# A hybrid decoder layer: row products moved from the first to the second attention pass, and a reordered seam in the MLP

## The chip, the cores and the metric

One core of a Trainium2 chip. The metric is the device time in microseconds of one execution, a median of several runs. The core has five engines with a queue of instructions each: TensorE (PE; its weight loads are shown apart as PEld), VectorE (DVE), ScalarE (ACT), GpSimd (POOL) and SyncE (SP, which here only issues DMAs).

## What is computed

One layer with a mixer and an MLP, both in float32. 512 tokens, 2048 columns, 16 heads of 64, 8192 hidden columns. Six rows of 2048 numbers modulate the layer ("modulation rows", 0 to 5 in the kernel):

```python
c_act = jax.nn.silu(c)
mod = c_act @ w_ada + b_ada                    # six rows of 2048
sh1, sc1, gt1, sh2, sc2, gt2 = split(mod, 6)
h = rms_norm(x, g_pre_mix) * (1.0 + sc1) + sh1
proj = h @ w_in                                # q, k, v, gates, recurrent branch
o_att = nsa_attention(...)                     # compressed, selected and window branch
o_rnn = gelu(yr) * rg_lru(conv(xr))
mix = concat(rms_norm(o_att), rms_norm(o_rnn)) @ w_out
x = x + gt1 * rms_norm(mix, g_post_mix)
h = rms_norm(x, g_pre_mlp) * (1.0 + sc2) + sh2
f = square(relu(h @ w_ff1)) @ w_ff2
x = x + gt2 * rms_norm(f, g_post_mlp)
```

`gt1` is row 2, `sh2` row 3, `sc2` row 4 and `gt2` row 5: none of the four is needed before the output projection is evaluated, the last one not before the end of the MLP.

## The kernel before, in words

**Precision.** A float32 operand is split into a high part (a copy by ScalarE in a shorter format) and a low part (the difference, by VectorE), and TensorE makes three products of them. So each weight tile costs ScalarE and VectorE a pass: lines 102 and 103 for the weights of the projections (class `Units`: SyncE loads `wr`, line 84, the split goes to `sl`), lines 1299 and 1300 (`part`) for those of the MLP (`fr`, loaded at line 1294, and sums of its blocks `fs`, lines 1315 to 1318). `AH` and `AL` are the two parts of the activations.

**Row products.** Modulation rows 2 to 5 are not matrix products on TensorE. `qdot` (lines 208 to 219) loads a 128x512 tile of `w_ada` into `md` (line 217), with a quarter of the activated condition in `ca` (line 216, one load for every 16 tiles), and VectorE multiplies and sums them in one instruction (line 218), which in the trace has two records, the product and the read of its sum. 64 such products make a row, 256 make the four. They are put in wherever the program calls `qdot`: in attention (rows 2, 4, 3 in this order), in the output projection (`cdots`, what is left of rows 4 and 3), and in the second MLP product (row 5, one for each step). `qvec` (line 221) adds up a row when it is complete.

**Attention.** `attention(pair, natoms)` runs twice, pass 0 and pass 1, over 64 units (head, branch, 128 query rows): scores on TensorE, a softmax row on VectorE (line 736) with the exponential on ScalarE, a reciprocal and a gate (lines 746, 747), transposes on TensorE, the split of the transposed probabilities (line 767), and the product with the values. Between them `fill` puts pieces of the remaining projections and of the recurrent branch. At the end of each step of the loop `nmod` grows by `MRATE`, 0.8, and a `qdot` is called for each whole unit:

```python
nmod[0] += MRATE
while nmod[0] >= 1:
    qdot(bp, 2 if QD[2] else 4 if QD[4] else 3, 1)
    nmod[0] -= 1
```

**Output projection.** Four blocks of 512 columns (`out_k`, `mmt`: lines 915 to 917), with `cdots` spreading the rest of the products over the first blocks, in the ring `tmp` of six buffers.

**MLP.** The first product (`group`) and the second (`f2_mm`) use a scheme of seven products for a 2x2 block, so that sums of weights and of activations are formed on VectorE. The loop at the end of the program goes over the groups `GR`: first those of ff1 (kinds "a", "b", "c", four groups for one pair of column blocks), then the steps of ff2 (kind "f"; `WIN` and `JOIN` say which pairs belong to which window k). When a pair of ff1 is complete, `pair_end` (lines 1392 to 1423) evacuates its banks, applies relu and square, and stores the seven sums to `ud` on GpSimd's queue. `u_load` (1434) reads them back as `uf` on the same queue, `u_form` (1444 on ScalarE, 1445 on VectorE) splits them into a slot of `AH` and `AL`. `bank_open` (1457) fills a bank of PSUM with zeros before ff2 accumulates in it, `bank_out` (1462) copies it out, `fin_step` finishes the last four windows. The "seam" is the passage from the last pair of ff1 to the first step of ff2; the last pair's `pair_end` runs there in pieces, one after each group.

**What sets the order.** The tile framework schedules the program: each engine has its own queue, filled in an order that follows the written one but is shifted by the framework's readiness estimates, and a buffer of a ring is reused when its last reader is done. A DMA stands in the queue of the engine that issues it, and what is behind it waits if it has to wait.

## Time and profile before

| | |
|---|---|
| runs | 2198.32 us median of 3 (2195.87 to 2200.69) |
| the profiled execution | 2199.99 us, span 2198.3 us |
| mean granted clock of TensorE | 0.982 |
| TensorE busy | 2093.1 us, 95% of the span |
| VectorE busy | 1879.1 us, 85% |
| ScalarE busy | 1392.2 us, 63% |
| GpSimd busy | 63.5 us, 3% |
| moved by DMA | 411.12 MB, 187 GB/s on average |

The share of a span says little of a stage: the page's 40 slices show stretches in which TensorE is busy throughout, and others where VectorE is. All times below are counted from the start of the span. The softmax rows of pass 0 run from 215.7 to 417.6 and those of pass 1 from 482.3 to 652.5; the output projection ends at about 870; the seam lies around 1530. "Granted clock" 1.00 is TensorE's upper level of 2.4 GHz and 0.50 the lower one, 1.2 GHz.

### The profile page before, as it was taken

The numbers are of one execution on the slowest core, as the hardware profiler recorded it, in microseconds if no ns is written. First come the engines' busy times: TensorE is split into PE (matmuls) and PEld (weight loads), VectorE is DVE, ScalarE is ACT, GpSimd is POOL, SyncE is SP. The second block draws the span as 40 slices with busy tenths as digits, with TensorE's granted clock in tenths as the row PEclk, the third lists the DMA queues.
The fourth block names the chain that finished last, engine by engine and source line by source line (L and its number), as shares of the span: only waits on it lengthen the run. The fifth ranks groups of instructions, "written<-read, shape, count | busy, mean of one in ns | idle before, by whom it ended". The sixth has DMA issues, their size and how long they took to land.

```text
span 2198.3 us, 39410 instructions
## 1 busy us (share of the span) xinstructions
PE 2093.1 (95%) x14621; PEld 1911.7 (87%) x14621; DVE 1879.1 (85%) x3764; ACT 1392.2 (63%) x2536; POOL 63.5 (3%) x119
## 2 busy tenths in 40 slices
PE   7998999989999989999999999998999999999995
PEld 3686777778877867899999999998999999999995
DVE  8987989877887677889999999999888887887788
ACT  4349879648995226765555555545766777767764
POOL 0000000000000000000000000000000000000010
PEclk9999999999999999999999999999999999999998
DMA  9764544762127886555555555566766544544453
GB/s 380 309 234 139 189 158 149 219 199 68 59 85 225 275 290 203 180 191 175 184 180 171 175 186 178 194 206 207 248 218 217 188 164 141 165 151 157 138 171 116
DMA packets 138818, 411.12 MB, mean 187 GB/s; under 512 B 18225, under 2 KB 25281, under 8 KB 134273
## 3 DMA queue, kind: packets, MB, share of 16 engines
q1 hardware_dynamic: 126178, 341.49, 46.6%
q0 software_dynamic: 12448, 67.12, 8.8%
q8 instruction: 115, 1.88, 0.4%
q14 instruction: 77, 0.63, 0.1%
HBM read 366.58 MB, written 41.97 MB: 186 GB/s over the span
## 4 chain that ended last, share of the span: by engine, by line
PE 52%; issue 26%; DVE 12%; ACT 5%; DMA 5%; POOL 0%; SPq 0%; DVEq 0%; POOLq 0%; ACTq 0%
PE ps_pj L1132 3%; PE ps_pj L1133 3%; PE ps_pj L1134 3%; DMA md<-wada 3%; DVE fl L1300 3%; PE ps_pj L1479 2%; PE ps_pj L1480 2%; PE ps_pj L1481 2%; PE ps_T L1132 2%; PE ps_T L1134 2%; PE ps_T L1133 2%; PE ps_S L1134 2%; PE ps_S L1132 2%; PE ps_S L1133 2%; PE ps_S L1479 2%
## 5 line engine op out<-in xcount | busy, mean ns | idle before, releaser
L1299 ACT ACTIVATE fh<-fs 128x1024 fp32r<-128x1024 f32 x256 | 272.9, 1066 | 324.7 <-DVE fs L1318 139.6
L1300 DVE TENSOR_TENSOR fl<-fs,fh 128x1024 fp32r<-128x1024 f32 x256 | 312.3, 1220 | 98.2 <-ACT fh L1299 95.7
L1299 ACT ACTIVATE fh<-fr 128x768 fp32r<-128x768 f32 (+2 forms) x296 | 217.1, 735 | 67.5 <-PE ps_pj L1133 13.3
L1300 DVE TENSOR_TENSOR fl<-fr,fh 128x768 fp32r<-128x768 f32 (+2 forms) x296 | 239.9, 814 | 11.3 <-ACT fh L1299 11.3
L102 ACT ACTIVATE sl<-wr 128x512 fp32r<-128x512 f32 (+2 forms) x252 | 145.6, 606 | 150.7 <-DMA wr<-wout 93.4
L218 DVE SCALAR_TENSOR_TENSOR md<-md,ca 128x512 f32<-128x512 f32 x256 | 171.4, 685 | 62.8 <-DMA md<-wada 39.7
L103 DVE TENSOR_TENSOR sl<-wr,sl 128x512 fp32r<-128x512 f32 (+2 forms) x252 | 163.6, 662 | 47.8 <-ACT sl L102 32.7
L1315 DVE TENSOR_TENSOR fs<-fr 128x512 f32<-128x512 f32 x256 | 175.2, 684 | 5.8 <-DMA fr<-wff 4.1
L1479 PE MATMUL ps_pj<-fh,AH 128*128 128x256 f32 x602 | 169.1, 281 | 1.1 <-ACT ps_pj L1459 1.0
L1480 PE MATMUL ps_pj<-fl,AH 128*128 128x256 f32 x602 | 169.1, 281 | 0.0
L1481 PE MATMUL ps_pj<-fh,AL 128*128 128x256 f32 x602 | 168.8, 281 | 0.0
L177 PE MATMUL ps_pj<-AH,sl 128*128 128x512 f32 x384 | 161.7, 421 | 0.1
L179 PE MATMUL ps_pj<-AH,sl 128*128 128x512 f32 x384 | 153.1, 399 | 0.7 <-DVE sl L103 0.7
L178 PE MATMUL ps_pj<-AL,sl 128*128 128x512 f32 x384 | 153.2, 399 | 0.0
L1479 PEld LDWEIGHTS ps_pj<-fh,AH 128*128 128x128 f32 x602 | 113.9, 189 | 2.1 <-ACT ps_pj L1459 2.1
L1480 PEld LDWEIGHTS ps_pj<-fl,AH 128*128 128x128 f32 x602 | 114.0, 189 | 0.4 <-DVE fl L1300 0.4
L1481 PEld LDWEIGHTS ps_pj<-fh,AL 128*128 128x128 f32 x602 | 114.0, 189 | 0.0
L1480 PE MATMUL ps_S<-fl,AH 128*128 128x256 f32 x394 | 110.4, 280 | 2.8 <-DVE fl L1300 2.8
L1479 PE MATMUL ps_S<-fh,AH 128*128 128x256 f32 x394 | 110.5, 280 | 1.3 <-ACT ps_S L1459 1.2
L1318 DVE TENSOR_TENSOR fs<-fs,fr 128x256 f32<-128x256 f32 x256 | 107.6, 420 | 3.5
L1481 PE MATMUL ps_T<-fh,AL 128*128 128x256 f32 x396 | 110.6, 279 | 0.0
L1479 PE MATMUL ps_T<-fh,AH 128*128 128x256 f32 x396 | 110.6, 279 | 0.0
(633 smaller groups left out, 7283.8 us busy)
## 6 DMA issues: line engine op xcount, KB each, us to landing
fr<-wff SPq DMA_DIRECT2D x276, 512.0 KB, 3.7
md<-wada SPq DMA_DIRECT2D x256, 256.0 KB, 4.3
uf<-ud POOLq DMA_DIRECT2D x32, 896.0 KB, 4.9
wr<-win SPq DMA_DIRECT2D x48, 512.0 KB, 3.7
ada<-wada SPq DMA_DIRECT2D x22, 1024.0 KB, 10.2
wr<-wout SPq DMA_DIRECT2D x36, 512.0 KB, 4.9
ud<-uf POOLq DMA_DIRECT2D x18, 896.0 KB, 5.2
ud<-uf POOLq DMA_DIRECT2D x14, 768.0 KB, 4.9
```

Source lines behind the costliest of these rows:

```text
L103: self.nc.vector.tensor_sub(lo, raw, self.f(hi))
L177: T.matmul(o, wh, mh, start=start, stop=False)
L218: (V.scalar_tensor_tensor(w, w, 0.5, CA[0], op0=OP.mult, op1=OP.mult, accum_out=dq[s_][:, q_, k:k + 1]))
L1132: T.matmul(o, wh, b[0], start=start, stop=False, skip_group_check=True)
L1133: T.matmul(o, wh, b[1], start=False, stop=False, skip_group_check=True)
L1134: T.matmul(o, wl, b[0], start=False, stop=stop, skip_group_check=True)
L1299: A.activation(hi, src, AF.Copy)
L1300: V.tensor_sub(lo, src, f(hi))
L1315: V.tensor_add(v2(Sm[:, :512]), v2(R[:, 256:768]), R[:, None, :256].to_broadcast([128, 2, 256]))
L1479: T.matmul(o, uh, hi, start=first and k < 4 and t_ == 0, stop=False, skip_group_check=True)
L1480: T.matmul(o, uh, lo, start=False, stop=False, skip_group_check=True)
L1481: T.matmul(o, ul, hi, start=False, stop=last, skip_group_check=True)
```

## The change

1. **Attention.** `MRATE` becomes a pair of rates, `MR = (0.4, 1.7)`: 0.4 calls of `qdot` per step in pass 0, 1.7 in pass 1. In pass 1 every fourth product takes its factor 0.5 not as a constant but from a fifth column of the current unit's `sm`, which a memset on VectorE fills just before; so the product depends on that tile.
2. **ff2.** Row 5 no longer goes through `qdot`. `q5_load` issues the loads of a product two steps ahead of `q5_dot`, with three buffers for `md` (two before) and two for `ca` (one before), from the window `KQ = 6` on. The store of the finished row and the load of `gbc2` that follows go from SyncE's to GpSimd's queue. The scratch `sq2` moves into the pool `gp`, which opens only then.
3. **Seam.** For the last pair the evacuation of the pair before it, the start of its own `pair_end` and the opening of the seven ff2 banks are written right behind its last group, ahead of the next weight load and of the split of the first activations.

```diff
--- before.py
+++ after.py
@@ -28,8 +28,9 @@
 Q_REST, K_REST, XR_T, YR_T = 0, 6, 8, 16
 
 
-NA1, NA2, NMS, NTMP, NXI, NPC, NSB, TD, MRATE, NMD, NRT = 4, 10, 22, 6, 4, 2, 11, 3, 0.8, 4, 6
+NA1, NA2, NMS, NTMP, NXI, NPC, NSB, TD, MR, NMD, NRT = 4, 10, 22, 6, 4, 2, 11, 3, (0.4, 1.7), 4, 6
 JOIN = [2, 1, 1, 1] * 5 + [2, 1, 1, 0, 3]
+KQ = 6
 HALF, CA_ = 512, 1
 PX = 0
 NB2 = 24
@@ -205,7 +206,7 @@
     CA = {}
     cad = dram.tile([1, D], F32, name="cad")
 
-    def qdot(pool, s_, n, ring=("md", NMD)):
+    def qdot(pool, s_, n, ring=("md", NMD), half=0.5):
         for _ in range(min(n, len(QD[s_]))):
             k, q_ = QD[s_].pop(0)
             w = pool.tile([128, S], F32, name="md", tag=ring[0], bufs=ring[1])
@@ -215,7 +216,7 @@
                 row = cad[0, S * q_:S * q_ + S]
                 nc.sync.dma_start(ca, bass.AP(tensor=row.tensor, offset=row.offset, ap=[[0, 128], [1, S]]))
             nc.sync.dma_start(w, wada[s_, k, :, S * q_:S * q_ + S])
-            (V.scalar_tensor_tensor(w, w, 0.5, CA[0], op0=OP.mult, op1=OP.mult,
+            (V.scalar_tensor_tensor(w, w, half, CA[0], op0=OP.mult, op1=OP.mult,
                                                             accum_out=dq[s_][:, q_, k:k + 1]))
 
     def qvec(o, s_, base=None, plus=0.0):
@@ -732,7 +733,7 @@
         n = 128 * (ch + 1)
         sp_ = UN[u][0]
         p_ = bp.tile([128, S], F32, name="pp", tag="pp", bufs=TD + 1)
-        sm = bp.tile([128, 4], F32, name="sm", tag="sm", bufs=6)
+        sm = bp.tile([128, 5], F32, name="sm", tag="sm", bufs=6)
         V.tensor_tensor_reduce(p_[:, :n], sp_[:, :n], mask[:, S - n:], scale=-0.125, scalar=3e38,
                                op0=OP.add, op1=OP.min, accum_out=sm[:, 0:1])
         A.activation(p_[:, :n], p_[:, :n], AF.Exp, bias=sm[:, 0:1], scale=-1.0, accum_out=sm[:, 1:2])
@@ -942,7 +943,7 @@
         add(lambda k=k: pre_out(k))
     n3 = len(stream)
 
-    nmod = [0.0]
+    nmod, ndot = [0.0], [0]
 
     def attention(pair, natoms):
         seq, info = [], {}
@@ -986,9 +987,14 @@
                 pv(u[0], u[1], i, PC[pair, ep])
                 if u[1] == 1:
                     head_out(u[0], i, t)
-            nmod[0] += MRATE
+            nmod[0] += MR[pair]
             while nmod[0] >= 1:
-                qdot(bp, 2 if QD[2] else 4 if QD[4] else 3, 1)
+                half = 0.5
+                if pair and get(s_) and ndot[0] % 4 == 0:
+                    half = UN[get(s_)][1][:, 4:5]
+                    V.memset(half, 0.5)
+                qdot(bp, 2 if QD[2] else 4 if QD[4] else 3, 1, half=half)
+                ndot[0] += 1
                 nmod[0] -= 1
         fill(natoms - done)
 
@@ -1480,6 +1486,24 @@
             T.matmul(o, uh, lo, start=False, stop=False, skip_group_check=True)
             T.matmul(o, ul, hi, start=False, stop=last, skip_group_check=True)
 
+    Q5, QC = {}, {}
+
+    def q5_load(i):
+        if i >= 64:
+            return
+        k_, q_ = QD[5][i]
+        if k_ == 0:
+            QC[q_] = OPP["p"].tile([128, S], F32, name="ca", tag="ca", bufs=2)
+            row = cad[0, S * q_:S * q_ + S]
+            nc.sync.dma_start(QC[q_], bass.AP(tensor=row.tensor, offset=row.offset, ap=[[0, 128], [1, S]]))
+        Q5[i] = OPP["p"].tile([128, S], F32, name="md", tag="md", bufs=3)
+        nc.sync.dma_start(Q5[i], wada[5, k_, :, S * q_:S * q_ + S])
+
+    def q5_dot(i):
+        k_, q_ = QD[5][i]
+        w = Q5.pop(i)
+        V.scalar_tensor_tensor(w, w, 0.5, QC[q_], op0=OP.mult, op1=OP.mult, accum_out=dq[5][:, q_, k_:k_ + 1])
+
     Y, XT, FIN = {}, {}, {}
 
     def fin_step(k, i):
@@ -1490,7 +1514,7 @@
         def done(t_, j, half):
             Y[n, j, half] = t_
             for c_ in range(2):
-                A.activation(sq2[:, c_], t_[:, 256 * c_:256 * c_ + 256], AF.Square,
+                A.activation(gbc2[1][:, c_], t_[:, 256 * c_:256 * c_ + 256], AF.Square,
                              accum_out=ssqf[:, 2 * j + c_, 2 * n + half:2 * n + half + 1])
             g_ = gbc2[0][:, None, 1024 * half + 256 * n:1024 * half + 256 * n + 256]
             V.scalar_tensor_tensor(v2(t_), v2(t_), (1.0, -1.0)[half], g_.to_broadcast([128, 2, 256]),
@@ -1555,7 +1579,6 @@
                 op_ = pool(ctx, "op")
                 for i in range(3):
                     p_tiles(op_, i)
-                sq2 = op_.tile([128, 2, 256], F32, name="sq2")
                 SL[4] = [(AHf[:, 7168:], ALf[:, 7168:]),
                          tuple(op_.tile([128, 768], F32R, name="us4" + x) for x in "hl")]
                 qst = ExitStack()
@@ -1600,20 +1623,33 @@
                 if g == pairs[-1] and k < NP - 1:
                     for i in (0, 2, 6):
                         x_tile(P[n][i])
-            if qn < 64:
+            if k >= KQ and qn < 66:
+                q5_load(qn)
+                if qn >= 2:
+                    q5_dot(qn - 2)
                 qn += 1
-                qdot(OPP["p"], 5, 1, ("md", 2))
-            elif qn == 64:
+            elif qn == 66:
                 qn += 1
                 qvec(gg2, 5, V_GQF)
-                nc.sync.dma_start(ggd[1].rearrange("o (a p) -> (o p) a", p=128), gg2)
+                G.dma_start(ggd[1].rearrange("o (a p) -> (o p) a", p=128), gg2)
                 qst.close()
-                gbc2[0] = pool(ctx, "gp").tile([128, D], F32, name="gbc2")
-                row_in(gbc2[0], ggd[1])
+                gp = pool(ctx, "gp")
+                gbc2[0] = gp.tile([128, D], F32, name="gbc2")
+                gbc2.append(gp.tile([128, 2, 256], F32, name="sq2"))
+                G.dma_start(gbc2[0], bass.AP(tensor=ggd[1].tensor, offset=ggd[1].offset, ap=[[0, 128], [1, D]]))
             continue
         if g == 2:
             pair_begin(q, kind)
         group(s)
+        if q == QO[-1] and g == 3:
+            for x in pe:
+                for _ in x:
+                    pass
+            pe = [pair_end(q, kind)]
+            next(pe[0])
+            next(pe[0])
+            for i in range(7):
+                bank_open(0, i)
         raw_load(s + 3)
         if s + 2 < len(GR) and GR[s + 2][0] != "a" and not RP:
             for _ in tg_:
@@ -1635,10 +1671,11 @@
                 alpha_end(q, BK.pop((kind, q))[0], ap_, "ax", 2)
             continue
         lastp = q == QO[-1]
-        for x in pe:
-            next(x, None)
-            if lastp:
+        if not (lastp and g == 3):
+            for x in pe:
                 next(x, None)
+                if lastp:
+                    next(x, None)
         if g == 0 and QO.index(q) and PORD[QO.index(q) - 1] == ("b", NA - 1):
             ast.close()
             xst = rst.enter_context(ExitStack())
@@ -1650,9 +1687,8 @@
             if lastp:
                 u_form(QO[0], "x")
                 u_load(QO[1])
-            pe = [pair_end(q, kind)]
-            next(pe[0])
-            if lastp:
+            else:
+                pe = [pair_end(q, kind)]
                 next(pe[0])
     rs = op_.tile([128, 4], F32, name="rsf")
     V.reduce_sum(rs, ssqf, axis=AX.X)
```

Lines of the changed kernel are higher by one in attention and by six in the MLP: 219, 737 and 768 are 218, 736 and 767 of before, and 1305, 1306, 1404, 1405, 1450, 1451 and 1463 are 1299, 1300, 1398, 1399, 1444, 1445 and 1457. Line 995 is the new memset, 1498, 1500 and 1505 are the loads of `ca` and `md` and the product in ff2.

VectorE in pass 1 before, in the middle of the pass: softmax rows (736, with its read), splits of probabilities (767), the normalisation (746, 747), and the convolution of the recurrent branch (805), no row product.

```order
L736 ISA pp,sm<-ps_S,mask 128x384
L736 ISA sm 128x1
L767 TENSOR_TENSOR ptl<-ps_T,pth 128x3x128
L805 SCALAR_TENSOR_TENSOR xc<-xp,vecs,xc 128x512
L746 RECIPROCAL sm<-sm 128x1
L805 SCALAR_TENSOR_TENSOR xc<-xp,vecs,xc 128x512
L747 TENSOR_TENSOR sm<-sm,gates 128x1
L736 ISA pp,sm<-ps_S,mask 128x512
L736 ISA sm 128x1
L805 SCALAR_TENSOR_TENSOR xc<-xp,vecs,xc 128x512
```

The same engine in pass 1 of the change, in its first part; 219 is the row product, 995 the memset into `sm`.

```order
L219 SCALAR_TENSOR_TENSOR md,dq_91<-md,ca 128x512
L747 RECIPROCAL sm<-sm 128x1
L219 SCALAR_TENSOR_TENSOR md,dq_91<-md,ca 128x512
L748 TENSOR_TENSOR sm<-sm,gates 128x1
L768 TENSOR_TENSOR ptl<-ps_T,pth 128x4x128
L737 ISA pp,sm<-ps_S,mask 128x512
L737 ISA sm 128x1
L104 TENSOR_TENSOR sl<-wr,sl 128x512
L995 MEMSET sm 128x1
L737 ISA pp,sm<-ps_S,mask 128x128
L737 ISA sm 128x1
```

Row products now stand between the softmax rows and the splits of pass 1.

VectorE at the seam before, from the split of the second activation tile (1445, `AL`) to that of the third; 1300 splits a weight, 1315 to 1318 are sums of weights, 1399 to 1405 evacuate the last pair of ff1.

```order
L1445 TENSOR_TENSOR AL<-uf,AH 128x1792
L1300 TENSOR_TENSOR fl_17133<-fs,fh_17132 128x1024
L1300 TENSOR_TENSOR fl_17189<-fr,fh_17188 128x768
L1315 TENSOR_TENSOR fs<-fr 128x512
L1399 TENSOR_TENSOR uf<-ps_T,uf 128x2x256
L1317 TENSOR_TENSOR fs<-fs,fr 128x256
L1402 TENSOR_TENSOR uf<-ps_S,uf 128x512
L1300 TENSOR_TENSOR fl_17191<-fs,fh_17190 128x1024
L1404 TENSOR_TENSOR uf<-ps_T,uf 128x2x256
L1405 TENSOR_TENSOR uf<-ps_S,uf 128x256
L1318 TENSOR_TENSOR fs<-fs,fr 128x256
L1445 TENSOR_TENSOR AL<-uf,AH 128x1792
```

The same place of the change.

```order
L1505 SCALAR_TENSOR_TENSOR md,dq_94<-md,ca 128x512
L1306 TENSOR_TENSOR fl_17238<-fr,fh_17237 128x768
L1321 TENSOR_TENSOR fs<-fr 128x512
L1405 TENSOR_TENSOR uf<-ps_T,uf 128x2x256
L1323 TENSOR_TENSOR fs<-fs,fr 128x256
L1408 TENSOR_TENSOR uf<-ps_S,uf 128x512
L1306 TENSOR_TENSOR fl_17240<-fs,fh_17239 128x1024
L1410 TENSOR_TENSOR uf<-ps_T,uf 128x2x256
L1411 TENSOR_TENSOR uf<-ps_S,uf 128x256
L1324 TENSOR_TENSOR fs<-fs,fr 128x256
L1321 TENSOR_TENSOR fs<-fr 128x512
L1451 TENSOR_TENSOR AL<-uf,AH 128x1792
```

The split of the second tile (now 1451) stood four rows ahead of line 1399 and now stands eight rows behind it (line 1405), and a row product (1505) stands ahead.

SyncE at the start of ff2 before: `ca` is the quarter of the condition, `md` the tile of a row product, `fr` the weights of the MLP, each row one DMA (or as many as it says).

```order
L1294 DMA fr<-wff 128x1024 x5
L216 DMA ca<-cad 128x512
L217 DMA md<-wada 128x512 x2
L1294 DMA fr<-wff 128x1024
L217 DMA md<-wada 128x512
L1294 DMA fr<-wff 128x1024 x2
L217 DMA md<-wada 128x512 x2
```

The same queue of the change.

```order
L1300 DMA fr<-wff 128x1024 x5
L1498 DMA ca<-cad 128x512
L1500 DMA md<-wada 128x512 x3
L1300 DMA fr<-wff 128x1024
L1498 DMA ca<-cad 128x512
L1500 DMA md<-wada 128x512
L1300 DMA fr<-wff 128x1024 x2
L1500 DMA md<-wada 128x512 x3
```

A second `ca` is loaded shortly behind the first, and three tiles of `md` stand ahead of the first weight load in place of two.

## Rows read from the trace of the kernel before

**Rows 1.** The page's first part: TensorE's busy time, share of the span, instructions.
```profile
PE 2093.1 (95%) x14621; PEld 1911.7 (87%) x14621; DVE 1879.1 (85%) x3764; ACT 1392.2 (63%) x2536; POOL 63.5 (3%) x119
```

**Rows 2.** Stretches: length; busy PE, PEld, DVE, ACT, POOL; granted clock; DMA share; GB/s.
```profile
215.70:417.60 201.90, 192.61 (x980) 155.34 (x980) 188.52 (x618) 166.82 (x394) 3.95 (x7) 1.00 0.55 173
417.60:482.30 64.70, 59.54 (x367) 52.56 (x365) 47.33 (x125) 25.62 (x52) 0.54 (x1) 0.98 0.72 237
482.30:652.50 170.20, 165.13 (x850) 134.44 (x849) 140.74 (x443) 152.51 (x360) 3.24 (x6) 0.99 0.21 66
...
738.00:870.00 132.00, 122.33 (x534) 95.67 (x533) 96.00 (x241) 52.90 (x124) 0.00 (x0) 0.96 0.77 257
1420.00:1525.00 105.00, 100.80 (x844) 99.96 (x843) 95.61 (x173) 54.82 (x76) 3.74 (x7) 1.00 0.67 222
1525.00:1560.00 35.00, 30.90 (x227) 30.20 (x226) 30.42 (x42) 25.71 (x43) 3.18 (x6) 0.85 0.67 238
1560.00:1740.00 180.00, 172.22 (x1451) 170.18 (x1450) 159.18 (x276) 124.32 (x186) 4.23 (x8) 1.00 0.64 209
1740.00:2100.00 360.00, 360.00 (x3079) 359.81 (x3078) 290.75 (x389) 262.52 (x373) 14.66 (x25) 1.00 0.48 159
...
672.00:805.00 133.00, 131.48 (x567) 104.59 (x567) 95.51 (x220) 42.81 (x83) 0.54 (x1) 1.00 0.82 276
```

**Rows 3.** The same stretches for line 218 alone: VectorE's busy us and rows.
```profile
215.70:417.60 201.90, 48.97 (x145) 1.00 0.55 173
417.60:482.30 64.70, 26.74 (x80) 0.98 0.72 237
482.30:652.50 170.20, 0.00 (x0) 0.99 0.21 66
...
738.00:870.00 132.00, 42.23 (x128) 0.96 0.77 257
```

**Rows 4.** VectorE's timeline (start, duration), then the group of line 805.
```profile
1543.83 0.68 DVE L218 SCALAR_TENSOR_TENSOR md<-md,ca 128x512 f32<-128x512 f32 x1
1544.44 0.07 DVE L218 DVE_READ_ACCUMULATOR md<-md,ca 128x1 f32 x1
...
L805 DVE SCALAR_TENSOR_TENSOR xc<-xp,vecs,xc x24: 742/749/753, 231.6 to 612.1; 128x512 f32<-128x512 f32 x24
```

**Rows 5.** TensorE's waits from 417.6 to 482.3 (total us, times, longest).
```profile
PE ps_pj L685 <- DVE qd L253: 4.0, 1, 4.0
```

**Rows 6.** TensorE's waits from 738 to 870, then SyncE's timeline.
```profile
PE ps_pj L915 <- ACT sl L102: 5.5, 3, 4.7
...
802.89 0.33 SPq L216 DMA_DIRECT2D ca<-cad  x1
...
804.76 0.38 SPq L84 DMA_DIRECT2D wr<-wout  x1
```

**Rows 7.** Stretches with the lower clock; columns as in Rows 2.
```profile
811.00:821.00 10.00, 5.65 (x12) 3.63 (x12) 8.56 (x20) 4.61 (x12) 0.00 (x0) 0.50 0.80 278
...
1531.00:1541.00 10.00, 7.79 (x35) 7.49 (x36) 8.46 (x11) 7.54 (x12) 0.53 (x1) 0.51 0.50 190
```

**Rows 8.** VectorE's waits from 1440 to 1740 (total us, times, longest).
```profile
DVE md L218 <- DMA md<-wada: 16.6, 16, 2.2
...
DVE md L218 <- DMA ca<-cad: 5.3, 3, 2.6
```

**Rows 9.** The seam, timelines of ScalarE, VectorE and TensorE, one row each.
```profile
1530.60 0.39 ACT L1457 ACTIVATE ps_T<-zz 128x256 f32<-128x256 f32 x1 [2.41 <-DVE uf L1399]
...
1525.34 2.02 DVE L1445 TENSOR_TENSOR AL<-uf,AH 128x1792 fp32r<-128x1792 f32 x1
...
1535.55 0.58 PE L1479 MATMUL ps_S<-fh,ush 128*128 128x256 f32 x1 [2.17 <-ACT ps_S L1457]
```

**Rows 10.** The store of `gg2` on SyncE, then a row of GpSimd's timeline.
```profile
DMA to landing us min/median/max: 11.3/11.3/11.3
...
1722.57 0.53 POOL L1434 DMA_DIRECT2D uf<-ud  x1 [21.20 <-DVE AL L1445]
```

## Prediction

> **What bounds the kernel now.** I read the page first: TensorE is busy for 95% of the span [rows 1], so a change can win only where TensorE waits or runs at the lower clock, and can lose wherever another engine becomes slower than TensorE's own work. Next the stretches [rows 2], cut at the first and last softmax row (line 736) of each attention pass and at the seam between the two MLP products. In pass 0 (215.7 to 417.6) VectorE is busy 188.52 of 201.9 us, 93%; TensorE is idle 201.9 - 192.61 = 9.3 us. In pass 1 (482.3 to 652.5) VectorE has 140.74 of 170.2 us and TensorE is idle 5.1. From 738 to 870, the output projection, TensorE is idle 9.7; in the three stretches from 1420 to 1740 it is idle 4.2, 4.1 and 7.8; from 1740 to 2100 not at all. Third, where the row products stand: two rows each in [rows 3], so 72 in pass 0, 40 between the passes, none in pass 1, 64 in 738 to 870; the 16 that are left of 192 lie between 652 and 738. Last, waits and queues [rows 5 to 9], which say what ended the idle time.
>
> The profiled execution took 2199.99 us with a span of 2198.3. The median of the three runs is 2198.32, so what I sum against the former is given 1.7 us lower at the end. About 0.2%, 4.4 us, can be told from no change.
>
> **Pass 1 gets the products.** The new order has 41 row products among the softmax rows of pass 0 (72 before), 0 between the passes (40), 95 in pass 1 (0), 20 from there to the first evacuation of the output projection (16) and 36 in its evacuations (64); both columns sum to 192. One product costs VectorE 0.61 us in a filled stream: it starts at 1543.83 and the next instruction at 1544.44 [rows 4]. So pass 1 gains 95 x 0.61 = 58.0 us on VectorE. A quarter of the products of this pass take their factor from a column of `sm`, which a new memset fills; I count 25 such memsets there. The nearest rows: a column that VectorE touches alone takes 0.07 us, like the read of the product's sum, and the existing instruction of this kind and shape with a factor from SBUF (line 805) 749 ns against 0.68 us [rows 4], so 25 x (0.07 + 0.07) = 3.5 us, a price well inside the ends below. VectorE then has 140.74 + 58.0 + 3.5 = 202.2 us of work where the whole pass lasts 170.2. Its rows stand in a fixed order, softmax rows behind products, and the scores and transposes of TensorE wait for those softmax rows; no other work fills the gap, since TensorE's order keeps its projections where they are.
>
> With no idle time on VectorE the pass is 32 us longer; at the share that VectorE reaches in pass 0 (0.934) it is 216.5, 46 longer. I take 0.96, between that and no idle time, because waits of VectorE for ScalarE and TensorE in pass 1 shrink when it is the late one: 210.6 us, **+40**. The loads of these products are no new bandwidth problem, since pass 1 moves 66 GB/s [rows 2]; on SP they stand ahead of weight loads, as in pass 0 today, and that is inside the 46.
>
> **What the other stages give back.** Pass 0 loses 31 products, 18.9 us of VectorE. What TensorE can gain is its idle time, 9.3 us; pass 1 shows 5.1 us of idle time with no product at all, so I take the difference, **-4**; ends 0 and -9.3.
>
> Here a rule speaks. The Trainium skill ("Perfetto Trace Analysis", Identifying the Most-Contended Engine) says that matmul busy time is a poor measure and that the busy share of weight loads tells the headroom. The row for 672 to 805, where 512-column matmuls run nearly without a pause (131.48 of 133 us), has the weight loads at 104.59, 79% [rows 2]; so 77% in pass 0 is close to full pace there and not a headroom of 23%. By the rule, pass 0 would be held by VectorE alone and return all 18.9 us; that is the second rival.
>
> Between the passes all 40 products go. TensorE is idle 5.2 us there, and 4.0 of them are one wait for line 253, an evacuation of queries on VectorE [rows 5]. I take **-4**; ends 0 and -5.2.
>
> In the output projection weights come late: a wait of 5.5 us in three parts for line 102 [rows 6], which needs a weight load. On SP a load of `ca` was issued at 802.89 and the weight load only at 804.76 [rows 6]; `ca` has one buffer, so its reload waits for the last product of the old quarter and holds what is queued behind. Then the clock: from 811 to 821 the granted clock is 0.50, the lower level, with 5.65 of 10 us busy [rows 7]. Together at most 9.7 + 5.1 (half of 10.2 us at the lower level) = 14.8 us. 28 of 64 products leave, the rest stay in bursts with weight loads between: 0.44 x 14.8, **-6**; ends 0 and -14.8. The four products more before that stage are 2.4 us on a VectorE that is not full; nothing, at most +2.4.
>
> **The MLP.** `KQ = 6` says that the last 64 products begin at the seventh step group. The built order does not follow: the first still stands at the 261st weight split of line 1300, as before, and the last one moves from the 371st to the 355th. What does change is the buffers, three for `md` and two for `ca`, with loads two products ahead. VectorE waited 16.6 us for `md` and 5.3 for `ca` between 1440 and 1740 [rows 8]. I take these as gone but for a fifth. TensorE is idle 4.2 + 7.8 = 12.0 us on both sides of the seam [rows 2], some of it behind ScalarE's bank evacuations that stay. I take two thirds, **-8**; ends 0 and -12.
>
> At the seam TensorE waits for zeroed banks. ScalarE's zero fill at 1530.60 had waited 2.41 us for line 1399 on VectorE [rows 9]; idle time 4.1 us, then the lower clock (0.51) from 1531 to 1541 [rows 7]; at most 4.1 + 5.3 = 9.4 us. In the new order line 1399 (now 1405) still stands behind two splits and a sum, with three products among the rows ahead in place of the split of the second activation tile (line 1445), which moves behind it. That split ran at 1525.34 for 2.02 us [rows 9]; now it is the eighth row behind line 1399. From 1525 to 1560 a row of VectorE takes 30.42 / 42 = 0.72 us [rows 2], so it begins near 1530.6 + 8 x 0.72 = 1536 and ends near 1538, while TensorE's products with that tile stood ahead of the idle 2.17 us that ended at 1535.55 [rows 9], so before 1533.4. One wait replaces another: **0**; ends -9.4 and +5.
>
> The store of `gg2` and load of `gbc2` go from SP to POOL. The load can start only when the store has landed, 11.3 us after its issue [rows 10]; TensorE shows no idle time there [rows 2], so nothing is gained. On POOL the load of the next activation tile stands behind them and can be 11.3 us late, but POOL sat idle 21.2 us before such a load [rows 10], and the tile before it is still unread; nothing is lost. If that cover were gone, the cost would be those 11.3 us once.
>
> **Sum.** +40 - 4 - 4 - 6 - 8 + 0 = +18: 2199.99 + 18 = 2218 in a profiled execution, **2216 us** as a median.
>
> **Rivals.**
> 1. *Everything else lets go* (faster). One mechanism: product loads in SP's queue hold the weight loads and keep VectorE late in all the other stages. Pass 1 costs only 32, because VectorE has no idle time; pass 0 returns 9.3, the middle 5.2, the projection 14.8, the MLP 12 and the seam 9.4, together 50.7: -19, or 2179 as a median. It decides where the give-back exceeds 32 us. For it: the waits for `md` and `ca` are real [rows 8]. Against: in the projection 36 products remain and the seam gets a new wait. 0.11.
> 2. *Pass 0 follows VectorE.* 93% busy, it may set the pace there, and 18.9 us come back in place of 4: +3, 2201, no difference to be told. The rule on weight loads would have it so; the trace does not agree, with 79% at full pace [rows 2]. 0.12.
> 3. *The lower clock in pass 1.* TensorE would have about 20% idle time there. The rows show the clock at the lower level behind a broken-up stretch (811 to 821 and 1531 to 1541, TensorE busy 57% and 78%) [rows 7]. Three such spells of 10.2 us, if on the path, cost 15 us: 2231. The Trainium skill ("TensorE: Matmul & The Clock Gate", HAM oscillation) also has idle gaps between bursts bring the lower clock again and again; no run so far shows whether the short gaps here do. 0.08.
> 4. *The MLP part does not do what it says.* The products stay where they were, three together in place of two hold the splits as long, and the seam's new wait costs 5: +18 + 8 + 5 = +31, 2229. 0.11.
>
> The forecast keeps 0.58.
>
> **How the numbers follow.** Slower is the forecast with rivals 3 and 4: 0.77. Within 0.2% is rival 2, 0.12. Faster is rival 1, 0.11. The range: on the low side pass 1 without idle time (32, so -8) and the give-back of the other stages 12 larger than taken, 2196; on the high side pass 1 at 46 (+6) and rival 4 nearly in full, 2232. That leaves out most of rival 1 and the far end of rival 3.
>
> **What would show it.** Right: from the first to the last softmax row of pass 1, some 210 us with VectorE busy over 95% and 95 products; pass 0 at 198, the middle at 61; waits of VectorE for `md` and `ca` between 1440 and 1740 (shifted by the change) under 6 us; one wait of TensorE at the seam for the split of the second activation tile. Wrong: pass 1 under 200 us, which would say that products cost VectorE less than 0.61 us or don't stand there; pass 0 under 190; or an output projection without the lower clock and without waits for weights.

## The result and the profile after

The changed kernel takes 2225.38 us, median of four runs (2218.64 to 2228.09), against 2197.46 of the kernel before (2195.87 to 2200.69): a ratio of 1.0117 with a 95% interval of 1.0099 to 1.0134, 27.9 us slower. Forecast were 2216 us (+18) with a range of 2196 to 2232. The profiled execution, at 2228.09 us with a span of 2226.4, is the slowest of the four; each table of times below rests on one profiled execution of a kernel.

The stretches of the changed kernel that answer to those of before [rows 2], between the same softmax rows and around the same places; the columns are length, busy time of PE, PEld, DVE, ACT and POOL, granted clock, DMA share and GB/s.

```profile
218.10:414.00 195.90, 188.51 (x966) 153.19 (x966) 172.50 (x550) 167.27 (x395) 3.96 (x7) 1.00 0.42 135
414.00:471.30 57.30, 57.30 (x355) 50.91 (x354) 23.51 (x46) 26.41 (x52) 0.54 (x1) 1.00 0.30 97
471.30:692.80 221.50, 189.39 (x883) 148.25 (x882) 196.50 (x663) 160.42 (x370) 3.80 (x7) 0.91 0.53 169
...
1548.00:1588.00 40.00, 31.18 (x239) 30.69 (x239) 32.09 (x54) 26.87 (x44) 3.19 (x6) 0.87 0.72 254
1588.00:1768.00 180.00, 173.08 (x1444) 171.87 (x1443) 156.62 (x260) 124.21 (x183) 6.49 (x11) 0.98 0.63 210
...
779.70:911.70 132.00, 130.22 (x623) 105.57 (x622) 88.16 (x207) 63.46 (x151) 0.00 (x0) 1.00 0.64 207
```

Pass 0 is 195.9 us long (201.9 before), the stretch between the passes 57.3 (64.7), pass 1 221.5 (170.2). The output projection's row, the last, shows TensorE busy for 130.22 of 132 us (122.33 before). The loss is in pass 1. VectorE's share there is 196.50 / 221.5 = 0.89, and TensorE, idle for 5.1 us before, is idle for 32.1; its busy time has grown from 165.13 to 189.39 as well, at a mean clock of 0.91. These stretches end at softmax rows, and the rows have moved against TensorE's work: pass 1 now holds 883 matmuls, 850 before. The table by matmul number below does not depend on that.

The row products in the changed kernel, line 219 alone, two rows each; they answer to [rows 3].

```profile
218.10:414.00 195.90, 27.92 (x82) 1.00 0.42 135
414.00:471.30 57.30, 0.00 (x0) 1.00 0.30 97
471.30:692.80 221.50, 65.44 (x190) 0.91 0.53 169
692.80:779.70 86.90, 13.27 (x40) 0.93 0.74 247
779.70:911.70 132.00, 23.39 (x72) 1.00 0.64 207
```

41, 0, 95, 20 and 36 products: just as the built order has it. To place a loss by stage, one engine can be followed: every trace here holds 14,621 matmul records, so the n-th of one kernel can be compared with the n-th of another. The table gives how much later (+) or earlier (-) TensorE got through each piece than in the kernel before; the times are those of before.

| matmul numbers (us in before) | changed | attention alone | MLP alone | row 5 only | half in pass 1 | even rates |
|---|---|---|---|---|---|---|
| up to 1650 (to 391, in pass 0) | +1.9 | +1.4 | +0.8 | -0.7 | -1.4 | +0.7 |
| to 2250 (508, start of pass 1) | -11.7 | -11.7 | -0.1 | -0.3 | -11.8 | -8.0 |
| to 3080 (679, end of pass 1) | +52.2 | +48.2 | -0.5 | +0.3 | +5.4 | +9.4 |
| to 3750 (848, output projection) | -14.6 | -14.7 | -0.9 | -2.9 | -2.5 | -10.0 |
| to 8900 (1479, first MLP product) | -0.1 | -2.8 | -0.5 | +0.2 | +0.3 | 0.0 |
| to 9200 (1520) | -3.7 | +0.2 | -5.3 | -3.8 | -4.5 | -5.0 |
| to 9290 (1537, seam) | +4.0 | -0.5 | +1.7 | +1.6 | +2.3 | +2.8 |
| to 10530 (1693) | -4.7 | +0.2 | -5.0 | -3.6 | -4.3 | -4.5 |
| to 10720 (1717, store of the row) | +5.0 | 0.0 | +1.3 | +8.8 | +3.8 | +2.2 |
| to the end | -0.3 | -0.1 | -0.2 | -0.2 | -0.2 | +0.1 |

The first line differs by 3 us between kernels, and by 1.5 between MLP alone and row 5 only, whose attention is that of before; so single steps of 1 or 2 us are not read. The last five lines sum to +0.3, -7.5, -2.9 and -4.4 us in the changed kernel, MLP alone, half in pass 1 and even rates, whose MLP code is the same: what the MLP gains is known to some 4 us from one execution, not better.

What VectorE waited for in pass 1 of the changed kernel (total us, times, longest). No such wait stands in pass 1 before, which had no product.

```profile
DVE md L219 <- DMA ca<-cad: 8.8, 5, 2.9
...
DVE md L219 <- DMA md<-wada: 3.1, 6, 0.9
```

What TensorE waited for there, those over 3 us; before, its longest sum was 1.5 us.

```profile
PE ps_T L756 <- DVE ptl L768: 6.1, 5, 2.3
PE ps_O L776 <- DVE ot L792: 5.3, 3, 3.1
PE ps_O L783 <- DVE ptl L768: 5.1, 5, 2.1
PE ps_T L756 <- DVE sm L748: 3.5, 3, 2.8
```

All of it is work of a softmax unit, late on VectorE: the split of the probabilities (768), the gate (748), a head's output (792); these four are 20.0 of the 32.1 us. Then the clock, in two pieces of the same pass (columns as above):

```profile
560.00:590.00 30.00, 25.02 (x111) 20.08 (x110) 24.61 (x87) 14.11 (x36) 0.54 (x1) 0.84 0.54 181
...
650.00:680.00 30.00, 23.95 (x97) 18.51 (x97) 26.13 (x81) 22.72 (x49) 0.54 (x1) 0.83 0.54 174
```

The broken-up stretch brings the lower level again and again, as the third rival had it, here for up to a third of a piece. Matmuls 2250 to 3080, the +52.2 us of the table, show its share: TensorE is busy for 185.87 us with them, 164.88 before, at a mean clock of 0.89 for 0.97. So 21 of the 52 us are longer busy time of the same matmuls and 31 are idle time. Whether the pass would be shorter at the upper level all through, or TensorE would only wait longer for VectorE, no run shows.

The held products and their memsets (ns, minimum, median, maximum), 27 where the prediction counted 25:

```profile
L219 DVE SCALAR_TENSOR_TENSOR md<-md,sm,ca x27: 730/746/753, 471.6 to 693.8; 128x512 f32<-128x512 f32 x27
...
L995 DVE MEMSET sm<- x27: 59/59/59, 471.5 to 692.8; 128x1 f32 x27
```

746 and 59 ns answer to the 749 and 70 that the prediction took from its nearest rows.

### The profile page after: what moved, and what is told of

It reads as the page before. It is cut to its first block, busy times and chain, and to the rows that moved or that the text cites. A ratio compares the mean times of both kernels' runs of the same rounds, so it can differ in the third digit from the quotient of the medians.

```text
span 2226.4 us, 39433 instructions
## 1 busy us (share of the span) xinstructions
PE 2108.8 (95%) x14621; PEld 1924.5 (86%) x14621; DVE 1875.6 (84%) x3791; ACT 1399.2 (63%) x2538; POOL 65.4 (3%) x121
## 4 chain that ended last, share of the span: by engine, by line
PE 66%; DVE 16%; DMA 9%; ACT 6%; issue 3%; DVEq 0%; SPq 0%; POOL 0%; ACTq 0%; POOLq 0%
PE ps_pj L1138 3%; PE ps_pj L1139 3%; PE ps_pj L1140 3%; DMA md<-wada 3%; PE ps_pj L1485 3%; PE ps_pj L1486 3%; PE ps_pj L1487 2%; DVE md L219 2%; PE ps_T L1140 2%; PE ps_T L1138 2%; PE ps_T L1139 2%; DVE fl L1306 2%; PE ps_S L1138 2%; PE ps_S L1139 2%; PE ps_S L1140 2%
## 5 line engine op out<-in xcount | busy, mean ns | idle before, releaser
L178 PE MATMUL ps_pj<-AH,sl 128*128 128x512 f32 x384 | 162.8, 424 | 3.5 <-ACT sl L103 2.3
L180 PE MATMUL ps_pj<-AH,sl 128*128 128x512 f32 x384 | 157.7, 411 | 1.0 <-DVE sl L104 1.0
L219 DVE SCALAR_TENSOR_TENSOR md<-md,ca 128x512 f32<-128x512 f32 x165 | 109.4, 684 | 26.0 <-DMA ca<-cad 13.9
L1486 PE MATMUL ps_T<-fl,AH 128*128 128x256 f32 x396 | 111.1, 281 | 0.4 <-DVE fl L1306 0.4
```

The source lines that it names most:

```text
L178: T.matmul(o, wh, mh, start=start, stop=False)
L180: T.matmul(o, wl, mh, start=False, stop=stop)
L1486: T.matmul(o, uh, lo, start=False, stop=False, skip_group_check=True)
```

## The experiments

Ratios are against the kernel before, measured on the same chip; a kernel with one run has one time and no interval.

**Attention alone.** The kernel before with the first part of the change:

```diff
+MR = (0.4, 1.7); sm = bp.tile([128, 5], ...); nmod[0] += MR[pair]
+half = UN[get(s_)][1][:, 4:5]; V.memset(half, 0.5)
...
```

> The attention part alone (rates 0.4 and 1.7, the held products), with the MLP of before. In the trace of the change TensorE's instructions stand 27.8 us late when the output projection ends and 28.0 late at the end of the program, so by my theory this kernel takes all of it: 2222 to 2230 us. Rival (the MLP part costs something that the two traces hide, since its gains and losses cancel only by chance): under 2218.

2222.73 us, ratio 1.0120 (1.0103 to 1.0137), inside the first range. In its pass 1:

```profile
470.70:687.10 216.40, 183.74 (x880) 142.76 (x878) 196.02 (x663) 159.66 (x370) 3.79 (x7) 0.94 0.53 172
```

This part makes the loss alone: 48.2 us lost in pass 1, 11.7 and 14.7 gained on either side. With the gain of the next run it would leave some 20 us for the changed kernel, which lost 27.9; the profiled execution of that one lost 4 us more in pass 1 and had no gain in the MLP, and why is not shown.

**The MLP part alone.** The changed kernel with one rate and no held product:

```diff
-MR = (0.4, 1.7)
+MR = (0.8, 0.8)
...
-if pair and get(s_) and ndot[0] % 4 == 0:
+if False:
```

> The MLP part alone (row 5 with its loads two ahead, the store on GpSimd, the reordered seam), with one rate of 0.8 in attention and no held product. By the trace of the change: gains of about 5 us ahead of the seam and 5 behind it, 5.5 lost at the seam and 7.5 around the store of the row: 2194 to 2202 us, no difference. Rival (the forecast's own -8 for this part, with a seam that costs nothing): 2186 to 2192.

2192.60 us, ratio 0.9980 (0.9970 to 0.9991): a gain of 5 us, between the two expectations. The table shows 10.3 us gained around the seam, 1.7 lost at it and 1.3 net around the store. In the changed kernel's profiled execution the same code gained 8.4 and lost 4.0 and 5.0 at these two places; so it shows no gain from the MLP.

**VectorE's work or the loads?** Two experiments on pass 1. In the first the products keep their loads and lose their work:

```diff
-V.scalar_tensor_tensor(w, w, half, CA[0], ...)
+V.scalar_tensor_tensor(w[:, :1], w[:, :1], half, CA[0][:, :1], ...)   # in pass 1
```

> The changed kernel with the products that attention calls in pass 1 cut to their first column: all loads, waits and memsets stay, VectorE's work on some 95 products goes (left out: the other 511 columns of these products, so the modulation rows are not whole). Theory (VectorE's work sets pass 1): pass 1 from 221 back to 168 to 180 us, the lower clock mostly gone from it, 2172 to 2186 in all. Rival (the loads of the products, `ca` with its one buffer above all, hold VectorE's queue): pass 1 stays over 200, and the whole over 2205.

2186.55 us. Pass 1, and VectorE's waits for the products' loads there:

```profile
466.90:652.90 186.00, 172.63 (x875) 137.76 (x873) 149.28 (x665) 153.76 (x361) 3.24 (x6) 0.98 0.61 198
...
DVE md L219 <- DMA md<-wada: 15.4, 19, 2.0
DVE md L219 <- DMA ca<-cad: 5.7, 4, 3.1
```

186.0 us, between the expectations. VectorE has only 149.28 us of work, 0.80 of the stretch, and the pass is still 16 us longer than before (22.8 us in the table's piece): VectorE waited 21.1 us for `md` and `ca`, and a softmax row behind a waiting product waits too, although the engine is idle. The second keeps the work and takes the loads:

```diff
+if keep is not None and len(keep) == 2:                  # in pass 1
+    V.scalar_tensor_tensor(keep[0], keep[1], half, CA[0], ...)
+    continue
...
```

> The changed kernel with the products of pass 1 made from one resident tile: VectorE's work stays (104 products in pass 1 by the order), some 100 loads of 256 KB and the reloads of `ca` go (left out: the right operands of these products). Theory (VectorE's work): pass 1 stays at 205 to 225 us, since only the 12 us of VectorE's waits for these loads can go. Rival (the loads): pass 1 falls to 170 to 185 us, the whole to 2185 or less.

2208.93 us. Pass 1 without the loads, with 104 products:

```profile
464.70:672.20 207.50, 183.26 (x880) 144.05 (x878) 200.12 (x680) 158.31 (x370) 3.78 (x7) 0.93 0.17 55
```

207.5 us, inside the theory's range, with VectorE busy for 200.12, a share of 0.964. So work alone, here even of 104 products, explains 37 of the some 50 us lost, the lower clock (0.93) included; the loads add the rest. The table's piece says the same: with 200.66 us of VectorE's work in both kernels it takes 208.4 us without the loads and 223.8 with them. Without the work the loads cost more (the 22.8 us above), so the two parts can't be added up.

**Two buffers for `ca` in attention**, paid with one of `md`:

```diff
-NMD = 4; ca: bufs=1
+NMD = 3; ca: bufs=2
```

> The changed kernel with two buffers for `ca` and three instead of four for `md` in attention. Theory (VectorE's work sets most of pass 1, and the wait for `ca`, 8.5 us, is a part by itself): pass 1 from 216 to 221 down to 208 to 213 us, 2211 to 2219 in all. Rival (the loads of `md` only come later instead): pass 1 at 215 or more.

2212.82 us once, inside the first range, but pass 1 (the table's piece: +47.3) says the rival:

```profile
466.90:682.70 215.80, 183.00 (x883) 141.51 (x881) 198.19 (x669) 160.57 (x370) 3.78 (x7) 0.95 0.55 177
...
DVE md L219 <- DMA md<-wada: 12.0, 19, 1.4
```

The 8.8 us for `ca` are gone and 12.0 for `md` stand in their place, against 3.1. What holds the loads of `md` is named in SyncE's waits of the attention-alone kernel:

```profile
SPq L217 <- DVE md L218: 87.1, 50, 6.9
```

By this row the next load stood in the queue 50 times, for 87.1 us in all, until a product had freed its buffer. Of the 15 us by which the whole beats the changed kernel's profiled execution only 5 lie in pass 1; 8 lie in the MLP, whose code is the same.

**How many products pass 1 takes.** Rates of 0.8 and 0.8, all of pass 1 still held:

```diff
-MR = (0.4, 1.7)
+MR = (0.8, 0.8)
```

> The changed kernel with rates 0.8 and 0.8, every product of pass 1 still held: 45 products in pass 1 by the order (95 in the change), 1 between the passes, 64 in the evacuations of the output projection as before. Theory (VectorE's work, 140.7 + 45 x 0.65 = 170 us at a share of 0.96 to 0.91): pass 1 at 177 to 187 us, between 24 products (175) and 95 (216 to 221); the projection gains nothing. Rival (a cost for each held product, in proportion: 48 us for 95): pass 1 at 191 to 195.

2187.20 us once. Pass 1:

```profile
468.50:643.00 174.50, 167.88 (x875) 135.15 (x873) 163.87 (x546) 152.56 (x361) 3.24 (x6) 1.00 0.41 133
```

Better than either expectation. With 45 products it lost 5.4 us in the table's piece and the stretch before it gained 11.8, since 39 products less stand between the passes. With 24 (below) it lost 5.0 and 6.9 in two kernels, with 15 2.2. So up to some 45 a product costs 0.1 to 0.3 us here; from 45 to 95 it is (48.2 - 5.4) / 50 = 0.86 us, more than its own 0.61 on VectorE. No run lies between 48 and 95 products, so where the price rises is not shown.

The MLP-alone kernel has the same rates without the hold, and its pass 1 has no product (42 stand between the passes). So at this rate it is the hold on `sm` that puts products into pass 1.

**The output projection.** Two buffers for `ca` there, in the kernel before:

```diff
-NTMP = 6; ca: bufs=1
+NTMP = 5; ca: bufs=2      # in the output projection
```

> The kernel before with two buffers for `ca` and five instead of six for `md` in the output projection, nothing else. Theory of the prediction (the reload of the one `ca` waits for the old quarter's last product and holds the weight loads behind it in SyncE's queue): the projection gains 5 to 14 us, 2184 to 2193. Rival (the number of products and of their loads there is what makes the weights late): within 3 us of before, 2195 to 2201.

2200.55 us once, the rival: TensorE's waits there, 9.3 us before for the weights' splits, are

```profile
PE ps_pj L916 <- DVE sl L103: 4.8, 2, 4.6
PE ps_pj L915 <- ACT sl L102: 2.4, 1, 2.4
```

7.2 us. The second `ca` was paid with a buffer of `md`, so what it would give alone is not shown. What counts is how many products stand there, as the runs of other rates show: the piece of the table gains 13.9 to 14.7 us with 36 or 41 products, 10.0 with 49, 5.5 with 52, and with 64 up to 2.9 (3.4 in this kernel).

**Row 5 only:** the MLP-alone kernel with the old seam and the store on SyncE.

```diff
-for i in range(7): bank_open(0, i)           # behind the last group
...
-G.dma_start(ggd[1]..., gg2); G.dma_start(gbc2[0], ...)
+nc.sync.dma_start(ggd[1]..., gg2); nc.sync.dma_start(gbc2[0], ...)
```

> Of the MLP part only the loads of row 5 two products ahead: the seam of before, the store of the row on SyncE, attention of before. In the MLP-alone kernel TensorE gained 3.0 us ahead of the seam and about 5 behind it, lost 1.7 at the seam and 3.4 around the store. Theory (the seam and the store are what takes the gain back): 2185 to 2190 us. Rival (the losses come from the denser products themselves): 2191 to 2196, with the same steps at the same instructions.

2198.80 us, ratio 1.0009 (0.9992 to 1.0025); neither expectation holds. The old seam loses the same 1.6 us, so the reordering of the seam shows no worth either way. The store on SyncE loses 8.8 us where GpSimd's lost 1.3 to 5.0:

```profile
1672.08 6.84 SPq L1300 DMA_DIRECT2D fr<-wff  x2
1679.09 0.38 SPq L1634 DMA_DIRECT2D ggd<-gg  x1
1690.83 0.33 SPq L1639 DMA_DIRECT2D gbc<-ggd  x1
...
DVE fs L1321 <- DMA fr<-wff: 9.2, 1, 9.2
```

These are SyncE's rows around the store, then VectorE's wait for the next weights, 9.2 us. The load of `gbc2` waits 11.7 us for the store with every weight load behind it, and only two tiles of weights had been sent ahead. In the kernel before the store came 53 us later, behind four, and TensorE lost nothing:

```profile
1718.63 12.96 SPq L1294 DMA_DIRECT2D fr<-wff  x4
1732.40 0.38 SPq L1609 DMA_DIRECT2D ggd<-gg  x1
```

Row 5 done earlier is what moved the store to where it hurts; that it hurts there because only two tiles were ahead is read from these rows and was not tried by itself.

**Few products in pass 1:** the run before (store on SyncE) with

```diff
-MR = (0.8, 0.8)
+MR = (0.8, 1.2)
...
-if False:
+if pair and get(s_) and ndot[0] >= 100 and ndot[0] % 4 == 0:
```

> Row 5 only, and in attention rates 0.8 and 1.2 with the held products only from the hundredth on: by the order 72 products in pass 0, 36 between, 24 in pass 1, 41 in the output projection's evacuations (64 before). Theory (pass 1 takes products for nothing until VectorE's work reaches 0.96 of the pass; here 140.7 + 24 x 0.65 = 156 of 170 us, 0.92): pass 1 at 168 to 174 us, the projection gains 8 to 14 us as in the change: 2174 to 2184. Rival (each product costs pass 1 its load's wait and its place ahead of a softmax row): pass 1 at 180 or more, 2188 to 2196.

2197.66 us, ratio 1.0002 (0.9988 to 1.0016). Its pass 1, with 24 products:

```profile
483.50:658.70 175.20, 166.10 (x848) 134.33 (x847) 153.19 (x502) 154.26 (x365) 3.25 (x6) 0.98 0.33 103
```

The projection gained 13.9 us, as the theory had it, but pass 1 with the stretch before it lost 7.5 and the store 8.4: neither expectation holds.

**The store held back:** the run before, with the store on GpSimd behind a late weight split.

```diff
+V.scalar_tensor_tensor(gg2, f(FM[s + 2][0][0][:, :16]), 0.0, gg2, op0=OP.mult, op1=OP.add)
-nc.sync.dma_start(ggd[1]..., gg2); nc.sync.dma_start(gbc2[0], ...)
+G.dma_start(ggd[1]..., gg2); G.dma_start(gbc2[0], ...)
```

> The kernel with few products in pass 1, with the store of row 5 and the load of `gbc2` on GpSimd and held back: one more instruction on VectorE adds zero times a weight split of the 90th step of ff2 to the row before it is stored. Theory (in the kernel without the hold TensorE was 12.1 us ahead of before until the store, and lost 8.4 there because weight loads came late beside it; 300 us later the store meets a stage with fewer loads): the 8.4 us stay, 2183 to 2189 us. Rival (the store costs the same wherever it stands): 2190 to 2198.

2193.34 us, ratio 0.9986 (0.9976 to 0.9995): the rival. The store, a weight load's landing (minimum, median, maximum) and VectorE's wait for weights, now near 1980:

```profile
1979.54 1.18 POOL L1635 DMA_DIRECT2D ggd<-gg  x1 [1.36 <-DVE gg L1634]
...
DMA to landing us min/median/max: 3.4/3.8/15.6
...
DVE fs L1321 <- DMA fr<-wff: 8.2, 1, 8.2
```

A weight load took 15.6 us beside it where 3.8 is the median, and TensorE lost 6.2 us there. Place and queue were changed together; on GpSimd at the old place the store had cost 1.3 to 5.0 us.

**Fifteen in pass 1:** the same with rate 1.0.

```diff
-MR = (0.8, 1.2)
+MR = (0.8, 1.0)
```

> As the run with the held store, with rate 1.0 in pass 1: 15 products in pass 1 and 52 in the evacuations of the output projection (24 and 41). Theory (the projection's gain has a point from which it comes, somewhere between 41 and 64 products): either all 13.9 us of it with pass 1 some 2 us shorter, 2181 to 2187, or none of it, 2194 to 2200. Rival (the gain is in proportion to the products taken out): about half of it, 2188 to 2193.

2198.39 us once, as a whole inside the theory's second range; but that is a loss of 7.5 us at the store, and the projection's piece gained 5.5 of the 13.9: its gain comes in parts, the rival.

**Even rates**, the version that beats both: the changed kernel with

```diff
-MR = (0.4, 1.7)
+MR = (0.95, 0.9)
```

> The changed kernel with rates 0.95 and 0.9 and nothing else: by the order 71 products in pass 0, 6 between the passes, 48 in pass 1, 49 in the evacuations of the output projection. From the run with 45 in pass 1 (2187.2 us once; pass 1 at 174, the stretch between the passes 13 us gained): 9 products more in pass 0, which cost nothing there in three kernels with 72; three more in pass 1, 2 to 3 us; the projection gains between the 5.2 us that it gained with 52 and the 13.9 with 41, where that run gained 2.0. Theory (pass 1 is free while VectorE's work, here 140.7 + 48 x 0.65 = 172 us, stays near TensorE's own 170): 2178 to 2189 us, faster than both kernels. Rival (some 45 held products already stand at the point from which each costs its full time): pass 1 over 180, 2190 to 2196.

2186.15 us (2182.05 to 2195.69, nine runs), ratio 0.9946 (0.9928 to 0.9965). Pass 1, with 48 products:

```profile
474.30:654.80 180.50, 170.28 (x876) 137.42 (x874) 166.27 (x553) 154.44 (x366) 3.24 (x6) 0.99 0.40 133
```

180.5 us, at the rival's bound, but the whole lies in the first range: 8.0 and 10.0 us gained ahead of and behind it are more than the 9.4 lost.

## Why the prediction was right

The time lies in the range, 9 us above the forecast, and the direction came for the reason given: pass 1 costs more than the other stages give back. That the sum came so near is in part luck: pass 1 cost more than its upper end and the stages on either side gave back far more than was taken, and these errors partly cancel. Of the prediction's own signs of being right, the 95 products and the new wait at the seam came; VectorE at over 95% of pass 1 (0.89) and waits for `md` and `ca` under 6 us (8.5, all for `md`) did not. One sign of being wrong came too: an output projection without the lower clock and without waits for weights.

**Pass 1: +40 taken, 46 to 52 measured**, beyond the upper end of 46. The mechanism held: 95 products, VectorE late, TensorE waiting for softmax work. Its work was put about right (202.2 us, measured 196.50). The term was too small because the loads were put "inside the 46". VectorE's share of 0.96 is what the pass reaches with no loads (0.964); with them it is 0.89 to 0.91. The failed step of this term is the sentence that they are no new bandwidth problem and so cost nothing of their own: bandwidth is not what they lacked (169 GB/s, where other stretches move up to 276 [rows 2]), but they wait for free buffers, and a product that waits for its load holds the softmax rows behind it in VectorE's queue. The third rival's lower clock came as well, and the forecast had no cost for it; in the attention-alone kernel the same pass took 216.4 us at a clock of 0.94, here 221.5 at 0.91.

**Pass 0: -4 taken, nothing to -3.4 measured.** 31 products less made no difference up to matmul 1650; of the step behind it, -3.4 us by 424 us of before, 2.1 were one wait for a split of probabilities (767), which is gone:

```profile
PE ps_O L782 <- DVE ptl L767: 2.2, 2, 2.1
```

So 18.9 us less of work on an engine busy for 93% gave TensorE almost nothing. The second rival, and the rule of the Trainium skill ("Perfetto Trace Analysis", Identifying the Most-Contended Engine) as weighed in the prediction, had all of it come back; the trace does not agree.

**Between the passes: -4 taken, about -8 measured** (the table's -11.7 begins in pass 0). The step bounded the gain by the idle time from 417.6 to 482.3. The wait for line 253 [rows 5], which it named, ended at 481, and TensorE ran at the lower clock behind it:

```profile
480.00:490.00 10.00, 8.87 (x34) 7.59 (x34) 8.30 (x26) 5.70 (x15) 0.00 (x0) 0.66 0.36 108
```

In the changed kernel both are gone (a clock of 1.00 from 471 to 500), and 6.7 us come back from 471 to 487 of before. The clock lies beyond the bound.

**Output projection: -6 taken, -14.6 measured.** "The rest stay in bursts" was the error: with 36 products no weight came late (TensorE's longest wait there is 0.7 us), and the lower clock did not come. The upper end of 14.8 was right.

**MLP: -8 taken, 10.3 gained and 3.0 given back** in one execution where it ran alone, some 5 by the ratio of ten runs (0 in all in the changed kernel's profiled execution). The wait for `md` fell from 16.6 [rows 8] to 8.9 us there, not to a fifth, and the one for `ca` went altogether.

**Seam: 0 taken, +1.7 to +4.0 measured**, with a new wait as forecast, at another place:

```profile
1546.47 0.53 POOL L1427 DMA_DIRECT2D ud<-uf  x1 [18.82 <-DVE fs L1324]
1553.36 0.54 POOL L1440 DMA_DIRECT2D uf<-ud  x1 [6.35 <-DMA md<-wada]
...
1560.65 1.70 ACT L1450 ACTIVATE AH<-uf 128x1792 fp32r<-128x1792 f32 x1 [6.77 <-DMA uf<-ud]
1562.25 0.37 ACT L1463 ACTIVATE ps_S<-zz 128x256 f32<-128x256 f32 x1
...
1562.67 0.58 PE L1485 MATMUL ps_S<-fh,ush 128*128 128x256 f32 x1 [7.76 <-ACT ps_S L1463]
```

Two rows of GpSimd, two of ScalarE, one of TensorE. The reload of the second tile's sums is issued 6.35 us behind the store of a pair, for which it waits (this row names another DMA; in the MLP-alone kernel the same wait, 4.96 us, names that store); ScalarE's split of them (1450) waits 6.77 us for the load, and the zero fill that TensorE needs (1463) stands behind the split. The prediction looked at VectorE's half of the split. The old seam behind the same products showed such a wait too (4.7 us), so the run with row 5 alone does not put it down to the reordering.

**The store: 0 taken, +1.3 to +5.0 measured on GpSimd, 8.8 on SyncE.** "Nothing is gained" and "nothing is lost" rested on the place that the store had before. In the changed kernel the store's issue, the landing of the weight loads from 1700 to 1720, VectorE's row and three stretches:

```profile
ggd<-gg POOLq DMA_DIRECT2D x1, 8.0 KB, 15.0
...
DMA to landing us min/median/max: 3.4/8.3/14.8
...
1725.19 0.69 DVE L1321 TENSOR_TENSOR fs<-fr 128x512 f32<-128x512 f32 x1 [5.30 <-DMA fr<-wff]
...
1712.00:1717.00 5.00, 5.00 (x45) 5.00 (x44) 4.15 (x5) 5.00 (x7) 0.00 (x0) 1.00 0.29 30
...
1725.00:1732.00 7.00, 3.26 (x15) 2.86 (x15) 6.78 (x10) 3.06 (x4) 1.00 (x2) 0.75 0.92 350
1732.00:1740.00 8.00, 8.00 (x58) 8.00 (x57) 7.01 (x11) 5.72 (x10) 0.00 (x0) 0.79 0.66 263
```

The store of 8 KB took 15.0 us; a weight load beside it took 14.8 us to land, while the core moved 30 GB/s (1712 to 1717); VectorE waited 5.3 for it; TensorE lost half of the next 7 us and ran at a clock of 0.75 to 0.79. The page "DMA: Bandwidth & Descriptors" of the Trainium skill (Rules for kernel authors) says that a transfer without a contiguous last dimension becomes one descriptor for each element; this store writes 2048 single elements. The trace of the kernel before, where SyncE issues it, agrees: 2081 packets of under 512 bytes from 1731 to 1744. Where GpSimd issues it, the trace of the changed kernel shows 65 such packets from 1708 to 1724, so that there it neither agrees nor refutes. No run here stores the row in another layout.

The sum, +18, was 10 us short of +28.0 in the profiled execution, with errors both ways: pass 1 cost 12 more, the MLP with seam and store 8 more, the stages on either side of pass 1 gave 12 more (26.3 for 14), and 1.9 lie ahead of all that was changed. The rival that was likeliest to mislead, that everything else lets go, was right about the projection, too low for the stretch between the passes and wrong about pass 1.

## What to carry to other kernels

Work that is shifted into a stage with idle time on its engine can be cheap while the engine's work stays near the stage's own length (here up to 166 us of VectorE's work in a pass of some 170 to 180), and cost more than its duration well beyond it (0.86 us for 0.61). What of that price is the loads, the chain over several engines that waits behind, or the lower clock, was not taken apart. Spread such work by measured counts for each stage, and look in the order for what holds it there. A load whose consumer stands in the same in-order queue as the critical work must be early, not only cheap in bandwidth. When something is finished earlier, look at what it triggers: a store that cost nothing in its old place can stall weight loads in the new one.

## What was not expected of the hardware

One 8 KB store, written element by element, slowed the other transfers of the core when GpSimd issued it: a 512 KB weight load beside it took 14.8 and 15.6 us in two kernels, where the medians around it are 8.3 and 3.8. It did so at two places 270 us apart. On SyncE it does not meet them in this way: the load of `gbc2` behind it holds the next weight loads back until it has landed. Why that cost TensorE nothing in the kernel before is explained here only in part, by the four tiles of weights that had been sent ahead; it was not tried by itself.
